# Both ends of a two-layer hybrid decode step rewritten: tokens in column halves ahead of the weights, last norm tile by tile

## The chip, the cores and the metric

One core of one Trainium2 chip runs the whole kernel. The metric is the device time of one execution in microseconds (us). The engines are PE (TensorE, matmuls; PEld is its weight load), DVE (VectorE), ACT (ScalarE), POOL (GpSimd) and SP (SyncE, which issues DMAs here). A matmul reads 128x128 stationary weights and a moving operand of up to 280 columns, the tokens.

## The reference, cut to what matters

A stack of two layers works on 272 prompt positions (16 of them meta tokens) and 8 decoded tokens, 280 columns, at width 1024. Each layer is a feed-forward block, three mixers side by side (S5, RWKV7, RG-LRU), and a second feed-forward block. The ends are what the change touches:

```python
meta = broadcast_to(meta_tokens, (bp, 16, 1024));  xp = concatenate([meta, x_prompt]);  xs = x_sample
for l in range(2):                       # for xp and xs alike
    h = h + 0.5 * swiglu(rmsnorm(h, ffn1_norm), w_gate, w_up, w_down)     # 1024 -> 2816 -> 1024
    h = h + mixers(rmsnorm(h, mix_norm) @ w_in) @ w_out
    h = h + 0.5 * swiglu(rmsnorm(h, ffn2_norm), w_gate2, w_up2, w_down2)
y_prompt = rmsnorm(xp, final_norm)[:, 16:];  y_sample = rmsnorm(xs, final_norm)
# rmsnorm(x, g) = x * rsqrt(mean(x*x) + 1e-6) * g
```

## The kernel before, in words

Activations lie transposed: width on the partitions in eight tiles j (KD = 8), tokens on the free axis. `hres` is the residual (8 tiles of 128x280, f32). For exactness every f32 operand is split in two parts of the type f32r: the activation into `xh` (made by ACT, times the norm's gain) and the residue `xl` (DVE), a weight piece of 128x4x128 into `whi` (ACT, L191) and `wlo` (DVE, L192). One product of a 128x128 weight block is three matmuls, xh by whi (L200), xl by whi (L201) and xh by wlo (L202). The reciprocal norm of a token is applied behind the product, so that a gemm needs the gains only.

Weights are loaded piece by piece (`wpiece`, L188, 256 KB from SP) into rings of five staging buffers, five whi and four wlo. A feed-forward block runs over 22 tiles of gate and up products, and then over eight output tiles j of the down product, each 66 matmuls of 264 columns in the last layer, where the meta tokens are left out (`ffn`, L313). After each the residual is added (L355, L356), its Square is added to `acc` (`acc_sq`, L257 to L261) and the next operand is split (`split_x`, L264, L265).

At the start five DMAs load the tokens as rows (L295 to L299), SP's three and ACT's two queues before the weights. The gains `pvst` are loaded and transposed to `pv` (`load_params`, L223 to L232). For each tile j the PE transposes the tokens into one PSUM bank (L306), DVE copies the bank into hres (L307), and `split_x` reads hres. PSUM has eight banks: psa three, psb two, psc two, psd one; a bank is free once its last reader is done. At the end ("fin", L1550 to L1575) six sums over partitions by `ones` (L1557) give the norm of each token, ACT scales the residual by the gain (`hg`, L1564), PE transposes it back (L1570), DVE multiplies by the norm (`yo`, L1571), and three DMAs store the rows.

A scheduler with a timeline model sets the order of instructions on each engine; `issue_after` ties one behind another. DMAs that SP and ACT issue share eight completion lanes in turn: an issue waits until the DMA eight before it has landed.

## Time and profile before

| | us |
|---|---|
| median of 3 runs | 1263.94 (1262.67 to 1265.52) |
| profiled execution | 1258.64, span 1256.8 |
| PE busy | 1211.6 (96% of the span) |
| DVE busy | 971.9 (77%) |
| ACT busy | 698.0 (56%) |
| POOL busy | 214.4 (17%) |
| chain that ended last | PE 83%, DVE 8%, DMA 4%, POOL 2%, issue 2%, ACT 1% |

The profile is of one execution; its span is the time from the first to the last recorded event. Busy shares are means over the whole span, and the two ends of a program have limits of their own, so the rows below are read by stretch. In rows of the timeline the first number is the start in us, the second the duration, then come the engine, the line, the operation, what is written and read, the tile and the count; in brackets stands the idle time of the engine ahead of it and what ended it. Consecutive matmuls overlap in these rows: the distance of two starts is the time that one costs.

### The profile page before, as it was taken

The numbers are of one execution on the slowest core, as the hardware profiler recorded it, in microseconds if no ns is written. First come the engines' busy times: TensorE is split into PE (matmuls) and PEld (weight loads), VectorE is DVE, ScalarE is ACT, GpSimd is POOL, SyncE is SP. The second block draws the span as 40 slices with busy tenths as digits, with TensorE's granted clock in tenths as the row PEclk, the third lists the DMA queues.
The fourth block names the chain that finished last, engine by engine and source line by source line (L and its number), as shares of the span: only waits on it lengthen the run. The fifth ranks groups of instructions, "written<-read, shape, count | busy, mean of one in ns | idle before, by whom it ended". The sixth has DMA issues, their size and how long they took to land.

```text
span 1256.8 us, 29154 instructions
## 1 busy us (share of the span) xinstructions
PE 1211.6 (96%) x10744; PEld 1154.9 (92%) x10744; DVE 971.9 (77%) x2345; ACT 698.0 (56%) x1529; POOL 214.4 (17%) x385
## 2 busy tenths in 40 slices
PE   7999999999898999999999999999999989999996
PEld 6999999988776999999998999998898779999996
DVE  7899957779687789985877778666876778877864
ACT  4466677564365556668544555457633656455543
POOL 2000000143443210000025000001615332500000
PEclk9999999989897999999999999999995989999998
DMA  7665654523311766554579656564423038965662
GB/s 184 170 184 161 178 145 142 164 83 107 96 29 55 187 165 183 171 170 129 155 203 240 184 169 171 171 176 128 119 79 82 2 87 226 244 196 170 190 187 83
DMA packets 376908, 187.47 MB, mean 149 GB/s; under 512 B 45532, under 2 KB 375352, under 8 KB 376766
## 3 DMA queue, kind: packets, MB, share of 16 engines
q1 hardware_dynamic: 376430, 184.47, 52.8%
q8 instruction: 84, 1.38, 0.5%
q10 hardware_dynamic: 336, 1.15, 0.3%
q14 instruction: 58, 0.48, 0.1%
HBM read 181.31 MB, written 3.37 MB: 147 GB/s over the span
## 4 chain that ended last, share of the span: by engine, by line
PE 83%; DVE 8%; DMA 4%; POOL 2%; issue 2%; ACT 1%; SPq 1%; DVEq 0%; ACTq 0%; POOLq 0%
PE psa L202 11%; PE psa L201 11%; PE psa L200 11%; PE psc L201 6%; PE psc L202 6%; PE psc L200 6%; PE psb L202 6%; PE psb L201 6%; PE psb L200 6%; PE psc L756 1%; DVE wlo L192 1%; PE psc L719 1%; PE psc L681 1%; PE psb L901 1%; DMA bc<-ds 1%
## 5 line engine op out<-in xcount | busy, mean ns | idle before, releaser
L191 ACT ACTIVATE whi<-stg 128x512 fp32r<-128x512 f32 (+2 forms) x664 | 400.7, 609 | 383.2 <-PE psa L201 101.3
L192 DVE TENSOR_TENSOR wlo<-stg,whi 128x512 fp32r<-128x512 f32 (+2 forms) x640 | 432.6, 682 | 129.2 <-ACT whi L191 29.9
L202 PE MATMUL psa<-xh,wlo 128*128 128x280 f32 (+1 forms) x930 | 274.1, 296 | 2.4 <-DVE wlo L192 2.3
L200 PE MATMUL psa<-xh,whi 128*128 128x280 f32 (+1 forms) x930 | 272.7, 294 | 2.0 <-DVE ts L1300 2.0
L201 PE MATMUL psa<-xl,whi 128*128 128x280 f32 (+1 forms) x930 | 273.0, 294 | 0.0
L202 PEld LDWEIGHTS psa<-xh,wlo 128*128 128x128 f32 x930 | 176.4, 190 | 6.0 <-DVE wlo L192 3.5
L200 PEld LDWEIGHTS psa<-xh,whi 128*128 128x128 f32 x930 | 177.1, 191 | 4.2 <-DVE ts L1300 2.2
L201 PEld LDWEIGHTS psa<-xl,whi 128*128 128x128 f32 x930 | 176.8, 190 | 1.6 <-issue 0.7
L201 PE MATMUL psc<-xl,whi 128*128 128x280 f32 (+1 forms) x498 | 144.6, 291 | 1.2 <-DVE xl L265 0.7
L202 PE MATMUL psc<-xh,wlo 128*128 128x280 f32 (+1 forms) x498 | 145.0, 291 | 0.7 <-DVE wlo L192 0.5
L200 PE MATMUL psc<-xh,whi 128*128 128x280 f32 (+1 forms) x498 | 144.8, 291 | 0.8 <-ACT xh L264 0.4
L202 PE MATMUL psb<-xh,wlo 128*128 128x280 f32 (+1 forms) x396 | 114.8, 290 | 1.0 <-DVE wlo L192 1.0
L200 PE MATMUL psb<-xh,whi 128*128 128x280 f32 (+1 forms) x396 | 115.0, 290 | 0.0
L201 PE MATMUL psb<-xl,whi 128*128 128x280 f32 (+1 forms) x396 | 114.8, 290 | 0.0
L201 PEld LDWEIGHTS psc<-xl,whi 128*128 128x128 f32 x498 | 94.0, 189 | 2.0 <-DVE xl L265 1.1
L202 PEld LDWEIGHTS psc<-xh,wlo 128*128 128x128 f32 x498 | 93.9, 188 | 1.7 <-DVE wlo L192 1.5
L200 PEld LDWEIGHTS psc<-xh,whi 128*128 128x128 f32 x498 | 93.9, 189 | 1.5 <-ACT xh L742 0.8
L202 PE MATMUL psb<-hh,wlo 128*128 128x280 f32 (+1 forms) x264 | 76.8, 291 | 0.0
L201 PE MATMUL psb<-hl,whi 128*128 128x280 f32 (+1 forms) x264 | 76.7, 291 | 0.0
L202 PE MATMUL psa<-hh,wlo 128*128 128x280 f32 (+1 forms) x264 | 76.5, 291 | 0.1
L200 PE MATMUL psb<-hh,whi 128*128 128x280 f32 (+1 forms) x264 | 76.7, 290 | 0.0
L201 PE MATMUL psa<-hl,whi 128*128 128x280 f32 (+1 forms) x264 | 76.6, 290 | 0.0
(620 smaller groups left out, 2578.7 us busy)
## 6 DMA issues: line engine op xcount, KB each, us to landing
stg<-in_ffn_w_gate_dram SPq DMA_DIRECT2D x176, 256.0 KB
stg<-in_ffn_w_up_dram SPq DMA_DIRECT2D x176, 256.0 KB
stg<-in_ffn_w_down_dram SPq DMA_DIRECT2D x160, 256.0 KB
stg<-in_w_in_dram SPq DMA_DIRECT2D x72, 256.0 KB
stg<-in_w_out_dram SPq DMA_DIRECT2D x32, 192.0 KB
bc<-ds SPq DMA_DIRECT2D x24, 192.0 KB
stg<-in_ffn_w_down_dram SPq DMA_DIRECT2D x32, 128.0 KB
bc<-ds SPq DMA_DIRECT2D x12, 256.0 KB
```

The costliest lines, as they stand in the source:

```text
L191: S.activation(hi[:, :kc], st[:, :kc], AF.Copy)
L192: (eng or V).tensor_tensor(lo[:, :kc], st[:, :kc], hi[:, :kc].bitcast(F32), op=SUB)
L200: PE.matmul(out, w[wk[i]][0], ah[:, k], start=(first and i == 0), stop=False)
L201: PE.matmul(out, w[wk[i]][0], al[:, k], start=False, stop=False)
L202: im = PE.matmul(out, w[wk[i]][1], ah[:, k], start=False, stop=(last and i == n - 1))
L681: PE.matmul(px[r][:, a], s5['xbt'][:, 4 * T + a, r], u4[:, 4 * T + a, 8:16 + NQ], start=True, stop=True)
L719: PE.matmul(py[32 * i:32 * i + 32, c0:c0 + n], w, x[:, o:NQ + ND], start=(m == 0), stop=(m == 2), skip_group_check=True, tile_position=(0, ...
L756: PE.matmul(pz[:, :NT], gw[k][:, j], z5[:, k, 0:NT], start=(k == 0), stop=(k == 2))
L901: PE.matmul(pg[h][:, hp], BK[r0, hp, c - 1].rearrange("p a t -> p (a t)"), RA[r0, hp, i, cs], start=True, stop=True)
```

## The change

At the start, the tokens are loaded by column halves, the first halves and the gains first, the weights behind the second halves. Nine matmuls of `ones` by itself into a psd bank run ahead of the transposes. xh (ACT) and xl (DVE) read the tokens' bank in PSUM, and the copies into hres come later: tile 0 behind the sixth xl, the other seven tied behind the wlo of the first four weight pieces, which are now made here and handed to the first `ffn` as `first`. The cast of `cidx` moves into `s5_prepare`, and the transposed final gain (`fgain`) goes.

At the end, "fin" becomes `final_norm`, which the last `ffn` calls. The final gain is loaded as a row broadcast to 128 partitions (`fg`, 512 KB) and scaled by POOL. After each output tile j of the last down product ACT squares the residual, PE adds three sums of one column over all eight tiles in one psd bank, and transposes the tile into three psa banks, four tiles to a bank; after tile 3 DVE multiplies the first half of the banks by fg. After tile 7 come the root, the scaling of the first halves (ACT) and the product of the second halves (DVE); four DMAs of 256 KB and a small one store the rows. The down product takes its banks from psb and psc in turn there, and the last `acc` isn't added up.

```diff
-        nc.sync.dma_start(xt[0][0:16], D['meta_tokens'])
-        nc.sync.dma_start(xt[0][16:128], xp[0:112])
-        nc.scalar.dma_start(xt[1], xp[112:240])
-        nc.scalar.dma_start(xt[2][0:16], xp[240:256])
-        nc.scalar.dma_start(xt[2][16:24], D['x_sample'].rearrange("b s d -> (b s) d"))
-        for _ in load_params(xin, PV_SPEC[:1]):
+        for c in (slice(0, DM // 2), slice(DM // 2, DM)):
+            nc.sync.dma_start(xt[0][0:16, c], D['meta_tokens'][:, c])
+            nc.sync.dma_start(xt[0][16:128, c], xp[0:112, c])
+            nc.scalar.dma_start(xt[1][:, c], xp[112:240, c])
+            if c.start == 0:
+                nc.scalar.dma_start(xt[2][0:16], xp[240:256])
+                nc.scalar.dma_start(xt[2][16:24], D['x_sample'].rearrange("b s d -> (b s) d"))
+                pv0 = load_params(xin, PV_SPEC[:1])
+                next(pv0)
+        pt = psD()
+        for _ in range(9):
+            PE.matmul(pt[:, :P], ones, ones, start=True, stop=True)
+        for _ in pv0:
             pass
...
         for j in range(KD):
             pt = psAB()
             for i, r in enumerate(rows):
                 PE.transpose(pt[:, P * i:P * i + r], xt[i][:r, P * j:P * j + P], ident[:r, :r])
-            V.tensor_copy(hres[:, j, :], pt[:, :NT])
-            split_x(j, gvec(0, 'ffn1_norm'), ALLC)
+            S.activation(xh[:, j], pt[:, :NT], AF.Copy, scale=g0[:, j:j + 1])
+            V.scalar_tensor_tensor(xl[:, j], pt[:, :NT], g0[:, j:j + 1], xh[:, j].bitcast(F32), op0=MUL, op1=SUB)
+            pts.append(pt)
+            if j == 5:
+                V.tensor_copy(hres[:, 0], pts[0][:, :NT])
+        for i in range(4):
+            w, iv = wpiece(wgu[i % 2][:, 4 * (i // 2):4 * (i // 2) + 4, 0:P], last=True)
+            first[i % 2] += w
+            for j in range(2 * i + 1, min(2 * i + 3, KD)):
+                with tc.issue_after(iv.ins):
+                    V.tensor_copy(hres[:, j], pts[j][:, :NT])
...
+    def final_norm():
+        groups = [(16, 128), (144, 128), (272, 8)]
+        fg = s5t.tile([P, DM], F32, name="fg", tag="k0")
+        nc.sync.dma_start(fg, D['final_norm'].unsqueeze(0).to_broadcast([P, DM]))
+        G.tensor_scalar(fg, fg, KR, None, op0=MUL)
...
+        def step(j):
+            sq = tmp("f", NRK)
+            S.activation(sq[:, 16:NT], hres[:, j, 16:], AF.Square)
+            for i, (c0, n) in enumerate(groups):
+                PE.matmul(ss[:n, i:i + 1], sq[:, c0:c0 + n], ones[:, 0:1], start=(j == 0 and i == 0), stop=(j == KD - 1),
+                          skip_group_check=True)
+            if j % 4 == 0:
+                pt[:] = [psA() for _ in groups]
+            for i, (c0, n) in enumerate(groups):
+                PE.transpose(pt[i][:n, P * (j % 4):P * (j % 4) + P], hres[:, j, c0:c0 + n], ident)
+            if j == 3:
+                for i, (c0, n) in enumerate(groups):
+                    V.tensor_tensor(yo[i][:n, half[0]], pt[i][:n], fg[:n, half[0]], op=MUL)
+            if j < KD - 1:
+                return
+            V.tensor_scalar(v[:, 0:2], ss[:, 0:2], 1e-6, None, op0=ADD)
+            V.tensor_scalar(v[:ND, 2:3], ss[:ND, 2:3], 1e-6, None, op0=ADD)
+            rsq(v, ry, rz)
+            for i, (c0, n) in enumerate(groups):
+                S.activation(yo[i][:n, half[0]], yo[i][:n, half[0]], AF.Copy, scale=ry[:n, i:i + 1])
+                V.scalar_tensor_tensor(yo[i][:n, half[1]], pt[i][:n], ry[:n, i:i + 1], fg[:n, half[1]], op0=MUL, op1=MUL)
+                for h, q in zip(half, (nc.scalar, nc.sync)):
+                    if i < 2:
+                        q.dma_start(yp[c0 - 16:c0 - 16 + n, h], yo[i][:n, h])
+            nc.sync.dma_start(ysm, yo[2][:ND])
...
-        acc2 = new_acc()
+        acc2 = new_acc() if gnext is not None else None
...
-                pd = psAB()
+                pd = psAB() if tail is None else (psB, psC)[j & 1]()
...
-                acc_sq(j, acc2, cols)
-                if gnext is not None:
+                if tail is None:
+                    acc_sq(j, acc2, cols)
                     split_x(j, gnext, cols)
+                else:
+                    tail(j)
```

How the instructions stand now is shown at three places. First SP at the start, before (xt are the tokens, pvst the gains, stg a weight piece, lw small weights of a mixer):

```order
L295 DMA xt_129<-in_meta_tokens_dram 16x1024
L296 DMA xt_129<-in_x_prompt_dram 112x1024
L223 DMA pvst_137<-in_ffn_norm_dram 8x2x128
L188 DMA stg<-in_ffn_w_gate_dram 128x4x128 x2
L188 DMA stg<-in_ffn_w_up_dram 128x4x128 [waits DMAHW0_49]
L188 DMA stg<-in_ffn_w_up_dram 128x4x128 [waits DMAHW1_49]
L188 DMA stg<-in_ffn_w_gate_dram 128x4x128 [waits DMAHW2_49]
L400 DMA lw<-in_rwkv_w_up_dram 64x384 [waits DMAHW3_49]
```

SP at the start, now:

```order
L289 DMA xt_127<-in_meta_tokens_dram 16x512
L290 DMA xt_127<-in_x_prompt_dram 112x512
L220 DMA pvst_135<-in_ffn_norm_dram 8x2x128
L289 DMA xt_127<-in_meta_tokens_dram 16x512
L290 DMA xt_127<-in_x_prompt_dram 112x512 [waits DMAHW0_49]
L187 DMA stg<-in_ffn_w_gate_dram 128x4x128 [waits DMAHW1_49]
L187 DMA stg<-in_ffn_w_up_dram 128x4x128 [waits DMAHW2_49]
L187 DMA stg<-in_ffn_w_gate_dram 128x4x128 [waits DMAHW3_49]
L187 DMA stg<-in_ffn_w_up_dram 128x4x128 [waits DMAHW4_49]
L187 DMA stg<-in_ffn_w_gate_dram 128x4x128 [waits DMAHW5_49]
```

The two weight pieces that went out without a wait now stand behind the second token halves, and each waits for a lane (DMAHW and a number). ACT issues its token loads, three before and four now, ahead of all its other work.

Second, DVE behind its constants, before (hres<- is the copy from PSUM):

```order
L151 CAST cidx<-cidxI 128x21
L192 TENSOR_TENSOR wlo<-stg,whi 128x512 x3
L232 COPY pv<-psd 128x8 x2
L307 COPY hres<-psb 128x280
L307 COPY hres<-psc 128x280
L307 COPY hres<-psa 128x280
L307 COPY hres<-psb 128x280
L192 TENSOR_TENSOR wlo<-stg,whi 128x512
L307 COPY hres<-psc 128x280
L307 COPY hres<-psa 128x280 x2
L265 SCALAR_TENSOR_TENSOR xl<-hres,pv,xh 128x280
```

The same place now, up to the copy that frees the bank (psc) that the first gemm writes:

```order
L226 COPY pv<-psd 128x8 x2
L312 SCALAR_TENSOR_TENSOR xl<-psb,pv,xh 128x280
L315 COPY hres<-psb 128x280
L312 SCALAR_TENSOR_TENSOR xl<-psc,pv,xh 128x280
L312 SCALAR_TENSOR_TENSOR xl<-psa,pv,xh 128x280
L312 SCALAR_TENSOR_TENSOR xl<-psb,pv,xh 128x280
L312 SCALAR_TENSOR_TENSOR xl<-psc,pv,xh 128x280
L312 SCALAR_TENSOR_TENSOR xl<-psa,pv,xh 128x280
L191 TENSOR_TENSOR wlo<-stg,whi 128x512
L322 COPY hres<-psc 128x280
```

The residues moved ahead of the copies, and the first weight piece's wlo behind six residues.

Third, PE at the end of the program, before (hg is the scaled residual, acc the squares' sum):

```order
L1570 MATMUL psa<-ident,hg 128x128
L1570 MATMUL psc<-ident,hg 128x128
L1570 MATMUL psa<-ident,hg 8x128
L1557 MATMUL psb<-ones,acc 128x1 x2
L1557 MATMUL psb<-ones,acc 8x1
L1570 MATMUL psb<-ident,hg 128x128 x4
```

PE now, in the middle of the last output tile's 66 matmuls, where the tile before it is finished:

```order
L201 MATMUL psc<-hh,wlo 128x264
L350 MATMUL psa<-ident,hres 128x128 x2
L350 MATMUL psa<-ident,hres 8x128
L199 MATMUL psc<-hh,whi 128x264
L200 MATMUL psc<-hl,whi 128x264
L345 MATMUL psd<-ones,tf 128x1 x2
L345 MATMUL psd<-ones,tf 8x1
L201 MATMUL psc<-hh,wlo 128x264
```

Three transposes and three sums of one tile now stand between the matmuls of the next, for tiles 0 to 6; the six of tile 7 are PE's last instructions. On POOL the scaling of fg stands between two steps of the second layer's S5 path that stood next to each other, behind a copy of an output state that now comes after them.

## Rows read from the trace of the kernel before

**Rows 1.** Busy time by stretches: stretch, us, each engine's busy us (count), granted clock.

```profile
0.00:20.00 20.00, 11.27 (x56) 10.07 (x57) 15.29 (x37) 11.00 (x24) 8.85 (x35) 1.00 0.78 191
1220.00:1240.00 20.00, 20.00 (x167) 20.00 (x166) 11.52 (x22) 8.53 (x16) 0.00 (x0) 1.00 0.45 132
```

**Rows 2.** Timeline of the first 19 us: SP, PE and DVE.

```profile
4.88 0.92 SPq L188 DMA_DIRECT2D stg<-in_ffn_w_up_dram  x2
7.35 0.66 PE L306 MATMUL psb<-ident,xt 128*128 128x128 f32 x2 [7.35 <-DMA xt<-in_x_prompt_dram]
10.50 0.38 PE L230 MATMUL psd<-ident,pvst 8*128 8x8 f32 x2
11.22 0.23 DVE L232 COPY pv<-psd 128x8 f32<-128x8 f32 x2
13.21 0.60 PE L200 MATMUL psc<-xh,whi 128*128 128x280 f32 x1 [0.43 <-ACT xh L264]
15.02 0.60 PE L201 MATMUL psc<-xl,whi 128*128 128x280 f32 x1 [0.73 <-DVE xl L265]
18.22 0.33 PE L201 MATMUL psc<-xl,whi 128*128 128x280 f32 x1
```

**Rows 3.** Chain that ended last, 0 to 30 us: start, us, what.

```profile
16.09 0.23 PE psa L201
...
20.08 0.13 PE psc L202
```

**Rows 4.** Timeline of DVE at the start: residues and a wlo.

```profile
12.80 0.68 DVE L192 TENSOR_TENSOR wlo<-stg,whi 128x512 fp32r<-128x512 f32 x1
...
17.65 1.33 DVE L265 SCALAR_TENSOR_TENSOR xl<-hres,pv,xh 128x280 fp32r<-128x280 f32 x3
```

**Rows 5.** DMA queues, 0 to 4 us: packets, MB, share; q10 is ACT's, q1 SP's.

```profile
q10 hardware_dynamic: 131, 0.52, 37.4%
q1 hardware_dynamic: 39, 0.09, 9.2%
```

**Rows 6.** Timeline of PE: sums and transposes inside streams of matmuls.

```profile
1055.34 0.63 PE L278 MATMUL psd<-ones,acc 128*128 128x1 f32 x6
...
1056.13 0.28 PE L200 MATMUL psc<-xh,whi 128*128 128x264 f32 x1
...
159.69 0.60 PE L637 MATMUL psd<-ident,bx 128*128 128x128 f32 x4
...
160.26 0.28 PE L201 MATMUL psb<-hl,whi 128*128 128x280 f32 x1
```

**Rows 7.** Timeline of the end, from the last gemm matmul to the stores.

```profile
1242.58 0.28 PE L202 MATMUL psb<-hh,wlo 128*128 128x264 f32 x1
...
1243.36 0.43 DVE L356 TENSOR_TENSOR hres<-tf,hres 128x264 f32<-128x264 f32 x1
...
1245.81 0.41 ACT L260 ACTIVATE tf<-hres 128x264 f32<-128x264 f32 x1
...
1247.06 0.63 PE L1557 MATMUL psb<-ones,acc 128*128 128x1 f32 x6
...
1249.90 0.75 DVE L1571 TENSOR_SCALAR yo<-psc,ry 128x512 f32<-128x512 f32 x1
...
1251.38 0.36 SPq L1573 DMA_DIRECT2D out_dram<-yo  x1
```

**Rows 8.** DMA from 1240 to 1257 us in 40 slices of 0.425 us.

```profile
GB/s 0 0 0 0 0 0 0 0 0 0 0 0 0 0 0 0 0 0 0 0 0 0 0 0 0 0 0 0 116 405 395 386 395 434 376 39 0 0 0 0
```

**Rows 9.** Timeline of the second mixers: POOL, and DVE's step before the S5 product.

```profile
1010.69 0.80 POOL L729 TENSOR_TENSOR tf<-tf 128x280 f32<-128x280 f32 x1
...
1013.78 0.44 DVE L731 SCALAR_TENSOR_TENSOR u<-tf 128x280 f32<-128x280 f32 x1
```

**Rows 10.** Chain, 380 to 420 us, and busy time of 397 to 398.

```profile
392.86 4.74 PE psc L756 x10
...
397.00:398.00 1.00, 1.00 (x6) 0.45 (x5) 0.69 (x2) 0.36 (x1) 0.00 (x0) 0.92 0.64 191
```

62 lines of the change are left out of this document (22 added, 40 removed).

## The prediction, made blind

> **What bounds the kernel now.** I read the busy time by stretches first. TensorE (PE) works 20.00 us of the 20 us from 1220 on, and 11.27 in the first 20 us [rows 1]. So PE is the bound in the feed-forward blocks, and two kinds of edit count at the ends: those that let the stream of matmuls start earlier or finish sooner, and those that put instructions into a stretch where PE has no idle time, which cost their full PE time there.
>
> Then the start, in order of time. SyncE's (SP) third weight load is issued at 4.88, since it waited for a token load to land. The first transpose runs at 7.35, when the tokens are there; the norm's gains (pvst) are transposed at 10.50 and copied from 11.22; the first gemm matmul starts at 13.21, does three matmuls, and the stream is only continuous from 15.02, where a matmul had waited 0.73 us for the residue xl [rows 2]. It runs at the lower clock at first: the chain of waits has a 280-column matmul every 0.23 us at 16.09 and every 0.13 us at 20.08 [rows 3], and the rows of the timeline change from the one to the other at 18.22 [rows 2]. These are the two levels, 280 columns at 1.2 and at 2.4 GHz. Sixteen matmuls stand before that change, so they cost 16 x 0.105 = 1.7 us more than at the upper level. Had the stream been continuous, it would have begun at 18.22 - 16 x 0.233 = 14.5, less 0.1 for its slower first matmul: 14.4. That is the number that the front has to beat.
>
> Last the end. From the start of the last gemm matmul at 1242.58 to the end of the span, 1256.8, are 14.22 us: the residual's add, a Square behind seven scalings on ACT (ScalarE), an add, the sums at 1247.06, the reciprocal root, six scalings from PSUM on DVE (VectorE) from 1249.90, and the stores, of which the first is issued at 1251.38 [rows 7].
>
> **The sum is made against the profiled execution**, 1258.64 us with a span of 1256.8; the median of the runs shown is 1263.94, 5.3 us above, and I take the same difference over to it.
>
> **Front: when the first operand is there.** The tokens' first halves (32 and 224 KB on SP, 256 KB on ACT), the 24-row tile and the gains are some 0.61 MB. The trace of before moves 0.61 MB by 4.0 us, both queues together [rows 5], and the end of the kernel shows 1.85 us from the last byte (1254.95, the last filled slice) to the end of the span [rows 8]. So they land at 5.85 if they go first. The row speaks against that: ACT's queue q10 had 0.52 MB by 4.0 us, SP's q1 0.09 [rows 5], so that ACT's second half, 256 KB, can go ahead of SP's first; at the 0.4 MB a us of the stores [rows 8] this is 0.65 us more, 6.5. The Trainium skill, DMA: Bandwidth & Descriptors, section Queues, rings and completion order, says that a DMA engine serves its queue rows in turn; by that they would land together at 5.85, and the trace here shows it only in part. I take 6.2, between the ends, because ACT's first half has a start of one issue in both kernels.
>
> On the same page, section Bandwidth, there is a rule that speaks against halving the loads: 1 MiB or more per DMA for three quarters of the peak. Its table has 138 GB/s at 64 KB and 341 at 1 MB; an estimate between them, 250 GB/s for 256 KB, would put the landing 0.8 us later and the whole sum 0.8 us higher. No row here has a load of 256 KB with 2 KB rows alone.
>
> From 6.2 the PE does eight transposes of 128 columns at 0.22 (fourteen from 7.35 to 10.50 [rows 2]), four of 24 columns, 0.4 in all, then the gains, whose copy starts 0.72 us after their transposes [rows 2]: 6.2 + 1.8 + 0.4 + 0.7 = 9.1 for the first xh. The first xl follows 0.5 later (an xh takes a little more than an xl), and DVE works through the order shown: six xl, a copy, the first wlo, and the copy that frees the bank of the first gemm. The eight of 280 columns cost 0.44 each (1.33 for three), the wlo 0.6 to 0.7 [rows 4]: 9.1 + 0.5 + 3.5 + 0.6 = 13.7. The second halves are due before 9.1 + 0.5 + 4 x 0.44 = 11.4, with the fifth xl; SP issues its own only when a lane is free, as at 4.88 before [rows 2], thus data by 6.6 and landing near 8.6: hidden. The weight pieces come after that; 256 KB at 0.9 us each, the first lands near 10, its whi is due on ACT after six xh, at 9.1 + 6 x 0.44 = 11.7: hidden, with 1.5 us in hand. The residual's copies and the sums of squares then lie beside a full PE. So the stream starts **0.7 us earlier** (14.4 - 13.7).
>
> The nine warm-up matmuls of ones are f32, two passes each, between 1 and 6 us, where PE has nothing else to do. Whether they change the clock, I bound from both sides: if it is up for all sixteen matmuls, 1.7 us are gained and the transposes before run at half, another 1.1; if the pause of over 4 us between the last transposes and the first gemm undoes it, nothing. Rows speak for both: in the mixer of layer 0 ten groups of such f32 matmuls from 392.86 run 4.74 us at the lower level, and in the slice at 397 the granted clock is 0.92 [rows 10], so this kind of work raises it; but the transposes of before, 7.35 to 12.5, were followed by a first gemm at the lower level [rows 2, 3]. I take half of the 1.7. **Front: -0.7 - 0.85 = -1.55 us**, from 0 to -0.7 - 1.7 - 1.1 = -3.5.
>
> **Last down projection.** For each of tiles 0 to 6 the change puts three sums of one column and three transposes between the next tile's matmuls, as the order shows. PE has no idle time there [rows 1], so they cost what they take. Three sums of the same form (six records) in a 264-column stream: from their start at 1055.34 to the matmul at 1056.13 are 0.79 us, and one other matmul, 0.12, lies between: 0.67 us. Four transposes, read in the same way: 159.69 to 160.26 is 0.57, less 0.12: 0.45, three 0.34 [rows 6]. Together 1.0 a tile, **+7.05 us for seven**, from 5.7 (0.3 for three transposes and 0.5 for the sums, without the hand-over) to 7.6 (0.63 and 0.45). Nothing waits for them: hres is ready 1.2 us after a tile's last matmul, its Square 1.7 (below), and they are queued half a tile, 4 us, later. The dropped DVE adds and ACT scalings gain nothing, since both engines had idle time there (DVE 11.52 of 20 [rows 1]).
>
> **Tail.** From the last gemm matmul's start: hres added at +1.21 (1243.36 + 0.43), Square, which now stands right behind it, 0.41 (1245.81 before): +1.7 and the sums start. Before, 2.84 us passed from the sums' start to the first product from PSUM (1247.06 to 1249.90), with three adds, the root's eight steps and a scaling; now there is one add and the scaling less, 0.1 and 0.2: +4.25. The product takes 0.75: +5.0 for the first SP store, while ACT scales its half beside it. Before, the first store was issued at 1251.38, +8.8 [rows 7]. Then the same 1.08 MB at 0.4 MB a us [rows 8]: data from +5.75 (the trace of before has the first bytes 0.8 after the issue) to +8.45, and 1.85 us: +10.3 in place of 14.22. **-3.9 us**, from -3.0 (the small store last) to -4.5.
>
> **Second mixers.** The POOL (GpSimd) now scales the 128x1024 gains before two steps of the path to the second S5 product. A 280-column operation takes 0.80 there, so it costs at most 1024/280 x 0.80 = 2.9, and I count it from nothing up. Most is hidden: POOL's last step ended at 1011.49, an activation of about 0.45 takes its result, and the DVE step behind that came only at 1013.78, so some 1.8 us are in hand [rows 9]. I take +0.4, from 0 to +1.0. The gains' load has idle DMA queues there.
>
> **Sum:** -1.55 + 7.05 - 3.9 + 0.4 = +2.0 us: 1260.6 for the profiled execution, **1265.9 on the median**. Its own range is 1263.5 to 1268.
>
> **The rivals.** Warm clock: front -3.5, the sum +0.05, 1264.0. For it speaks [rows 10], against it the pause.
>
> Faster: beside the warm clock, half of the inserted work is hidden, since a sum is one column and its cost is nearly all weight load, which runs beside matmuls. Then 7 x 0.5 = 3.5 and the sum is -3.5 + 3.5 - 3.9 + 0.4 = -3.5: 1260.4. Against it speak [rows 6], where the same insertions cost their full time. It decides below 0.6 us a tile.
>
> Slower: the weights are late. All pieces now wait for tokens to land, five of them one lane after another; if the first whi starts after 12 (1.5 us in hand used up) and each of the next comes 1 us late, the stream stalls at its first pieces, front +1.5 in place of -1.55: the sum +5.05, 1269.0. For it speaks SP's wait at 4.88 [rows 2].
>
> The change doesn't do what it says: the first gemm is no earlier, and the clock is low when it starts. Front 0, the sum +3.55, 1267.5.
>
> **How the numbers follow.** Forecast 0.42, warm clock 0.20, faster 0.17, weights late 0.14, front without effect 0.07. About 0.2%, 2.5 us (1261.4 to 1266.5), is what a measurement of this kernel can tell from no change. The forecast's range lies two thirds within it and one third or a little more above, the warm clock's nearly all within: faster 0.20, same 0.42, slower 0.38. The range reaches from 1260.0, the faster rival, to 1269.5, the late weights.
>
> **What would show it.** In the trace of after: first xh near 9.1, first gemm near 13.7 and without gaps behind it, spacing 0.23 or 0.13 there; whi of the first piece near 11.7; between the matmuls of the last down projection a loss of 1.0 us at each of seven tiles; about 10.3 us from the last tile's last matmul to the end; the second S5 product at most 1 us later behind its mixer. I am wrong if the seven insertions cost less than 0.6 each, or if the mixers, which the scheduler has reordered in a few rows, move by over 2 us.

## The result, and the profile after

| | before | after |
|---|---|---|
| median, us | 1262.67 (1259.68 to 1265.52, 5 runs) | 1272.45 (1269.24 to 1275.8, 5 runs) |
| ratio to before | | 1.0084 (95%: 1.0061 to 1.0106) |
| span of the profiled execution | 1256.8 | 1269.7 |

The change makes the kernel slower, by 7.7 to 13.4 us of 1262.67. The prediction was 1265.9, 1260.0 to 1269.5: too low, and the time lies outside its range. Of its terms the last down projection and the tail came out nearly as worked out; the front gained even more than was said, and none of it reached the end.

First the page of after, engines and the chain's shares. The table ahead of the prediction has 1211.6 us for PE:

```profile
PE 1223.1 (96%) x10804; PEld 1165.1 (92%) x10804; DVE 964.3 (76%) x2336; ACT 696.0 (55%) x1524; POOL 217.3 (17%) x385
...
PE 84%; DVE 7%; DMA 5%; ACT 2%; issue 1%; POOL 1%; SPq 0%; DVEq 0%; ACTq 0%
```

PE is busy 11.5 us more, in a span 12.9 us longer.

**The start.** Timeline of after, PE and ACT, to be held against [rows 2]:

```profile
1.12 4.21 PE L300 MATMUL psd<-ones 128*128 128x128 f32 x18 [1.12 <-DVE ones L114]
...
5.57 0.41 PE L310 MATMUL psb<-ident,xt 128*128 128x128 f32 x2 [0.24 <-DMA xt<-in_x_prompt_dram]
...
7.34 0.49 ACT L311 ACTIVATE xh<-psb,pv 128x280 fp32r<-128x280 f32 x1 [3.34 <-DVE pv L226]
...
7.89 0.60 PE L310 MATMUL psc<-ident,xt 128*128 128x128 f32 x3 [0.78 <-DMA xt<-in_x_prompt_dram]
...
11.93 0.57 PE L199 MATMUL psc<-xh,whi 128*128 128x280 f32 x1 [1.04 <-ACT xh L311]
...
15.09 0.43 PE L200 MATMUL psa<-xl,whi 128*128 128x280 f32 x1
...
15.33 0.35 PE L199 MATMUL psc<-xh,whi 128*128 128x280 f32 x1
```

The first halves of the tokens are there at 5.57 (forecast 6.2), the first xh starts at 7.34 (9.1) and the first gemm matmul at 11.93 (13.7; 13.21 before). The clock follows in the windows of after (stretch, us, each engine's busy us and count, granted clock, DMA share, GB/s):

```profile
5.20:8.60 3.40, 2.37 (x20) 1.82 (x19) 0.97 (x4) 1.26 (x4) 1.55 (x11) 1.00 1.02 272
...
8.80:15.20 6.40, 5.36 (x22) 4.42 (x22) 6.40 (x16) 5.95 (x15) 2.98 (x4) 0.50 0.72 187
...
1200.00:1220.00 20.00, 20.00 (x170) 19.80 (x169) 9.33 (x17) 8.47 (x15) 0.00 (x0) 1.00 0.62 181
```

The nine warm-up matmuls raise the clock for the transposes (1.00 from 5.2 to 8.6, the level of 2.4 GHz). Then PE stands for 0.78 us, since the second halves of the tokens land only at 7.89, and from 8.8 to 15.2 the clock is 0.50, the level of 1.2 GHz: the last transposes run there, and with them the first fourteen matmuls of the stream, up to the row at 15.33, behind which the steps are 0.13 us in place of 0.23. Before there were sixteen. The last window, from 1200 to 1220, belongs to the down projection: PE is busy for all of its 20 us.

**The last down projection.** Timeline of PE in after, one tile's insertion:

```profile
1200.11 0.28 PE L200 MATMUL psc<-hl,whi 128*128 128x264 f32 x1
1200.23 0.49 PE L350 MATMUL psa<-ident,hres 128*128 128x128 f32 x3
1200.47 0.37 PE L201 MATMUL psc<-hh,wlo 128*128 128x264 f32 x1
1200.68 0.63 PE L345 MATMUL psd<-ones,tf 128*128 128x1 f32 x6
1201.23 0.39 PE L199 MATMUL psc<-hh,whi 128*128 128x264 f32 x1
1201.46 0.28 PE L200 MATMUL psc<-hl,whi 128*128 128x264 f32 x1
```

From the first to the last of the four gemm matmuls are 1.35 us, where three steps of 0.12 would be 0.36: 1.0 us for this tile, the predicted price.

**The tail.** Timeline of after from the last gemm matmul, to be held against [rows 7]:

```profile
1258.91 0.28 PE L201 MATMUL psc<-hh,wlo 128*128 128x264 f32 x1
...
1260.17 0.42 ACT L343 ACTIVATE tf<-hres 128x264 f32<-128x264 f32 x1 [7.87 <-DVE hres L413]
...
1260.64 0.73 PE L345 MATMUL psd<-ones,tf 128*128 128x1 f32 x6
...
1263.24 2.06 DVE L361 SCALAR_TENSOR_TENSOR yo<-psa,nrm,fg 128x512 f32<-128x512 f32 x3
...
1264.02 1.02 SPq L364 DMA_DIRECT2D out_dram<-yo  x2
```

The sums start 1.73 us after the last matmul, the first product at 4.33, the first SP store is issued at 5.11, and the span ends at 10.8 (1269.7 - 1258.91); before these were 4.48, 7.32, 8.80 and 14.22 [rows 7]. The stores' bytes, DMA of after from 1255 to 1270 us in 40 slices of 0.375 us:

```profile
GB/s 0 0 0 0 0 0 0 0 0 0 0 0 0 0 0 0 0 0 0 0 0 0 0 0 0 0 240 399 355 377 393 371 388 350 11 0 0 0 0 0
```

They run from 1264.75 to 1267.75, 5.8 to 8.8 us behind the last matmul (forecast 5.75 to 8.45), and 1.95 us pass from there to the end.

**Where the time went.** The kernels compute the same 7584 gemm matmuls, so I count them from the first, matmul 0, and compare the time at which the n-th starts, in each trace (us from the span's start, as in the timeline). Matmul 1655 is the last of the first feed-forward block, 2015 the last of the first w_in product, 5807 of the second w_in, 7055 the last ahead of the last down projection.

| stretch, us | before | again | front alone | tail alone | after | again |
|---|---|---|---|---|---|---|
| first gemm matmul at | 13.21 | 13.27 | 11.71 | 13.26 | 11.93 | 12.01 |
| 0 to 100 | 16.5 | 17.3 | 15.4 | 16.0 | 15.2 | 15.5 |
| 100 to 1655 | 212.6 | 212.6 | 216.4 | 212.5 | 213.5 | 214.8 |
| matmul 1655 at | 242.3 | 243.2 | 243.4 | 241.8 | 240.6 | 242.2 |
| 1655 to 2015 | 78.4 | 75.4 | 75.9 | 76.9 | 77.4 | 75.4 |
| first mixers' end | 78.1 | 84.6 | 84.1 | 83.1 | 81.7 | 82.2 |
| 2016 to 5447 | 461.8 | 462.3 | 464.7 | 463.5 | 464.9 | 467.4 |
| 5447 to 5807 | 76.0 | 77.0 | 76.0 | 78.5 | 76.0 | 78.4 |
| second mixers' end | 83.5 | 79.7 | 85.7 | 83.1 | 85.7 | 82.3 |
| 5808 to 7055 | 158.4 | 159.5 | 159.7 | 162.3 | 161.5 | 162.8 |
| 7055 to 7583 | 64.07 | 64.07 | 64.07 | 71.16 | 71.11 | 71.11 |
| last gemm matmul to the end | 14.2 | 15.7 | 14.1 | 10.6 | 10.8 | 10.8 |

The trace that the prediction was made from has the shortest first mixers of all: 78.1, where the seventeen others of this study have 80.8 to 85.0. Of the 12.9 us between the two spans 3.6 are that.

### The profile page after: what moved, and what is told of

It is laid out like the page before. It is cut to its first block, busy times and chain, and to the rows that moved or that the text cites. A ratio compares the mean times of both kernels' runs of the same rounds, so it can differ in the third digit from the quotient of the medians.

```text
span 1269.7 us, 29260 instructions
## 1 busy us (share of the span) xinstructions
PE 1223.1 (96%) x10804; PEld 1165.1 (92%) x10804; DVE 964.3 (76%) x2336; ACT 696.0 (55%) x1524; POOL 217.3 (17%) x385
## 4 chain that ended last, share of the span: by engine, by line
PE 84%; DVE 7%; DMA 5%; ACT 2%; issue 1%; POOL 1%; SPq 0%; DVEq 0%; ACTq 0%
PE psa L201 11%; PE psa L200 10%; PE psa L199 10%; PE psc L201 7%; PE psc L200 7%; PE psc L199 7%; PE psb L201 6%; PE psb L200 6%; PE psb L199 6%; DMA stg<-in_ffn_w_gate_dram 2%; PE psc L779 1%; DVE wlo L191 1%; PE psc L741 1%; PE psb L961 1%; PE psc L816 1%
## 5 line engine op out<-in xcount | busy, mean ns | idle before, releaser
L191 DVE TENSOR_TENSOR wlo<-stg,whi 128x512 fp32r<-128x512 f32 (+2 forms) x640 | 431.6, 681 | 133.9 <-ACT whi L190 30.3
L201 PE MATMUL psb<-hh,wlo 128*128 128x280 f32 (+1 forms) x286 | 83.4, 292 | 0.2 <-DVE wlo L191 0.2
L199 PE MATMUL psb<-hh,whi 128*128 128x280 f32 (+1 forms) x286 | 83.2, 291 | 0.3 <-ACT whi L190 0.3
L200 PE MATMUL psb<-hl,whi 128*128 128x280 f32 (+1 forms) x286 | 82.9, 290 | 0.0
L201 PEld LDWEIGHTS psb<-xh,wlo 128*128 128x128 f32 x396 | 74.3, 188 | 1.6 <-DVE wlo L191 1.6
L199 PEld LDWEIGHTS psb<-xh,whi 128*128 128x128 f32 x396 | 74.5, 188 | 0.0
```

The lines of the kernel that those rows point to most:

```text
L191: iv = (eng or V).tensor_tensor(lo[:, :kc], st[:, :kc], hi[:, :kc].bitcast(F32), op=SUB)
L199: PE.matmul(out, w[wk[i]][0], ah[:, k], start=(first and i == 0), stop=False)
L200: PE.matmul(out, w[wk[i]][0], al[:, k], start=False, stop=False)
L201: im = PE.matmul(out, w[wk[i]][1], ah[:, k], start=False, stop=(last and i == n - 1))
```

## Experiments

Three theories stood against one another. **T1:** the front's lead is lost in the first feed-forward block, where the weights are handed over at DVE's pace, whenever PE starts. **T2:** the tail pays a second time outside its own stretch, by the scaling of the gain on POOL (GpSimd) or by another order of the mixers. **T3:** neither edit does it; dropping `fgain` moves every later tile in SBUF by 32 bytes, and DMAs run slower for it.

**Each end by itself.** The front alone keeps before's end, the section "fin" (diff against after):

```diff
-                else:
-                    tail(j)
...
-                pd = psAB() if tail is None else (psB, psC)[j & 1]()
+                pd = psAB()
...
+    with tc.tile_pool(name="fin", bufs=1) as fp:
```

> The front of the change alone; the last norm is that of the kernel before. In the two traces the stream of gemm matmuls runs 3.0 us earlier after the front, but the first layer's mixers take 3.6 us more and some feed-forward stretches lose 0.6 to 1.4 us each. Theory A (order): the front's other order of instructions in the first layer causes the mixers' loss each time, so this kernel is -3.0 + 3.6 + about 2 = 2 to 3 us slower than before. Theory B (chance): mixers and stretches vary from run to run whatever the kernel, so this kernel is 3 us faster, ratio 0.9975, and its first mixers may take 78 or 82 us.

Measured 1265.92 us, 1.0026 of before (1.0005 to 1.0046): +3.3 us, 0.6 to 5.8. The prediction's -1.55 is excluded.

The tail alone puts `final_norm` on the kernel before and leaves its start as it was (diff against after):

```diff
-        for c in (slice(0, DM // 2), slice(DM // 2, DM)):
-            nc.sync.dma_start(xt[0][0:16, c], D['meta_tokens'][:, c])
...
+        nc.sync.dma_start(xt[0][0:16], D['meta_tokens'])
+        nc.sync.dma_start(xt[0][16:128], xp[0:112])
```

> The tail of the change alone; the start is that of the kernel before. Down projection +7.05 and tail -3.5 are in both theories. Theory A (order, with the scaling of the final gain on POOL in the second mixers): second mixers +2.2 and the stretches behind them up to +2.5, so 6 to 8 us slower than before. Theory B (chance): 3.5 us slower, ratio 1.003.

Measured 1270.31, 1.0047 (1.0023 to 1.0071): +5.9 us, 2.9 to 9.0, where the prediction's three terms make +3.55, which lies within that interval. The two ratios together make 1.0073, after's is 1.0084: the ends add up, and no interplay is needed.

Both kernels once more, for a second trace of each (no edit):

> The kernel before again, for a second trace. Theory A (order): both mixers take 78.1 and 83.6 us between the gemms around them as in the first trace, to 0.5 us, and the clock's low stretches lie in the same places. Theory B (chance): they differ from the first trace by 2 us or more.

> The changed kernel again, for a second trace. Theory A (order): both mixers take 81.7 and 85.7 us as in the first trace, to 0.5 us. Theory B (chance): they differ from it by 2 us or more.

Measured 1263.32 and 1274.33; their stretches are the columns "again". The first mixers are shorter in before by 3.6 us in the one pair and longer by 2.4 in the other, so they tell nothing of the change.

**T1: the front's lead.** The front alone starts matmul 100 at 27.1 us, 2.7 earlier than the kernel before (29.7), and has lost that at matmul 1655 (243.4 and 242.3). The waits of PE from 15 to 250 us by what was waited for (in total, times, longest), first before:

```profile
PE psa L202 <- DVE wlo L192: 0.6, 1, 0.6
```

and the front alone:

```profile
PE psa L201 <- DVE wlo L191: 2.3, 3, 1.4
...
PE psb L201 <- DVE wlo L191: 0.9, 2, 0.7
PE psb L199 <- ACT whi L190: 0.3, 1, 0.3
```

PE waits 2.9 us more for weights being split. The longest, in the timeline of the front alone (POOL, DVE, PE):

```profile
51.35 1.41 POOL L434 MEMSET sta<- 32x1536 f32 x1 [37.19 <-DVE stsh_in L438]
...
51.35 1.43 DVE L464 TENSOR_SCALAR smlr<-pv 128x2 f32<-128x2 f32 x1
...
51.78 1.28 DVE L191 TENSOR_TENSOR wlo<-stg,whi 128x512 fp32r<-128x512 f32 x2
...
52.88 0.40 PE L201 MATMUL psa<-xh,wlo 128*128 128x280 f32 x1 [1.36 <-DVE wlo L191]
```

A DVE operation of two elements a partition takes 1.43 us: it starts and ends with POOL's clearing of `sta`, and the wlo that PE waits for stands behind it. The Trainium skill, Trainium Architecture — The Big Picture, section What this means for kernel authors, says that DVE and GpSimd share a port pair under an exclusive lock; the two rows that start together at 51.35 agree, 1.43 and 1.41 us.

So I cleared `sta` once a layer in place of five times, on the front and on the kernel before:

```diff
+        sta = tp.tile([32, 12, 4, 32], F32, name="sta", tag="sta")
+        G.memset(sta, 0.0)
...
-            a = tp.tile([32, 12, 4, 32], F32, name="sta", tag="sta")
-            G.memset(a[:, :nt], 0.0)
+            a = sta
```

> The front alone, and the staging tile of the decode state (sta) cleared by POOL once a layer in place of five times. In the eight traces with the front the stretch from the 100th to the 700th gemm matmul takes 79.3 to 82.4 us, with one to three stalls of 0.9 to 1.7 us where POOL's memset of sta (1.4 us) and a DVE step of two elements that takes 1.43 us lie side by side and the next wlo comes late; in the five without it 79.6 to 79.8, with one such stall. Theory (the memsets hold DVE up, and the front's order puts them where a wlo is due): 78.4 to 79.3 here, and the lead of 2.7 us at the 100th matmul is kept to the 1000th. Rival (the order itself, other DVE steps ahead of wlo): 81 or more, and the lead is gone by the 700th.

> The kernel before with the one memset of sta a layer, as the measure for the run with the front. Theory (memsets): 78.4 us from the 100th to the 700th in place of 79.7, total 1 to 2 us faster, ratio 0.999. Rival: 79.7 as before, no difference.

Measured 1263.74, 1.0008 (0.9989 to 1.0027) with the front, and 1261.47, 0.9998 (0.9975 to 1.0021) without. From matmul 100 to 700 the kernel before goes from 79.7 to 78.5 us (79.6 to 79.8 in seven traces without the front, 78.5 in both with a single clearing). With the front it goes from 82.2 to 81.0, but traces of the front with five clearings lie from 79.3 to 82.2 there, so that step could be chance. What the runs do show is that with a single clearing the front still takes 81.0 and 81.2. The clearing is a cost of both kernels and not what makes the front lose. (With the edit the scheduler also writes DVE's steps in another order.) What is left with the front, timeline of DVE and PE of that run:

```profile
49.16 2.17 DVE L440 STREAM_TRANSPOSE stsh_in<-sta 32x352 f32<-32x352 f32 x4
...
51.44 0.16 DVE L466 TENSOR_SCALAR smlr<-pv 128x2 f32<-128x2 f32 x1
...
51.87 1.28 DVE L191 TENSOR_TENSOR wlo<-stg,whi 128x512 fp32r<-128x512 f32 x2
...
52.60 0.40 PE L201 MATMUL psa<-xh,wlo 128*128 128x280 f32 x1 [0.94 <-DVE wlo L191]
```

The operation that took 1.43 us beside the clearing takes 0.16 without it, but PE still waits for the wlo behind it. The kernel before has the same four transposes of the states, in the timeline of DVE:

```profile
45.76 2.17 DVE L419 STREAM_TRANSPOSE stsh_in<-sta 32x352 f32<-32x352 f32 x4
...
48.47 1.28 DVE L192 TENSOR_TENSOR wlo<-stg,whi 128x512 fp32r<-128x512 f32 x2
```

and there no matmul waits behind them. The pace there is DVE's, as the windows show, first of before:

```profile
60.00:110.00 50.00, 50.00 (x390) 49.94 (x389) 48.66 (x204) 29.67 (x55) 0.60 (x2) 1.00 0.64 182
```

and the front alone:

```profile
60.00:110.00 50.00, 49.09 (x378) 48.79 (x379) 48.40 (x202) 28.81 (x54) 1.06 (x3) 1.00 0.62 176
```

DVE works 48.7 and 48.4 of these 50 us, in both kernels. It makes the wlo and does the state transposes and scalings of the mixers besides; PE is full too in before, but with the front it does 12 matmuls fewer in the same time, since it waits. From the end of a piece's wlo to the start of the first matmul that reads it, the first four pieces have 5.9 to 8.6 us before and 1.1 to 2.7 with the front; from the eighth to the fifteenth piece both have 3.5 to 5.1; and between the 24th and the 32nd both come down to 0.1. Two facts together speak for DVE: a start that is 2.8 us earlier for PE at matmul 100 is gone by matmul 1655 (242.6 on the mean of seven traces with the front, 242.5 of seven without, all with five clearings; the first trace of after alone still has 1.7 us there), while the four clearings that no longer hold up DVE shorten the way from matmul 100 to 1655 by 1.3 +- 0.4 us, by a fit over all 18 traces, with and without the front. And the loads aren't late there: from 60 to 110 us DVE waits 1.4 us in all with the front, none of it for a piece of weights. So the traces bear T1 out for this part: PE is fed at DVE's pace, and PE's start doesn't set it. It isn't shown by itself, since the scheduler also wrote DVE's steps in another order with the front, and no run has the one without the other. (Which of DVE's other steps the front makes PE wait for differs from trace to trace; no run moved them one by one.)

That covers about 1.7 us of the loss, up to matmul 700 (108.6 on the mean with the front, 109.7 without: 1.1 of the lead are left). The rest, 1.2, lies from matmul 1000 to 1500: 74.9 to 75.0 us with the front as the change has it, 73.6 before, with the same 78 matmuls and transposes of other kinds in between, which the scheduler put at other places. DVE isn't full there (50.47 of 65 us before, from 110 to 175). Three waits for pieces being split (wlo, whi, wlo) are 0.7 us of it, in each trace of this front, and before has none; why these come late is open.

**The clock.** What the front could gain from it, two runs show. One takes the nine warm-up matmuls away:

```diff
-        pt = psD()
-        for _ in range(9):
-            PE.matmul(pt[:, :P], ones, ones, start=True, stop=True)
```

> The front alone without the nine warm-up matmuls. Theory (they gain time only on the transposes, since the clock falls again before the first gemm): transposes of 128 columns take 0.21 in place of 0.11, the first gemm starts 1 us later than with them, near 12.7, and the 20th 1 us later too, near 17. Rival (they matter for the stream): the clock rises 2 us or more later, the 20th at 18 or later.

The other adds fourteen where PE would pause, behind the transposes of tiles 3, 6 and 7:

```diff
+            if j in (3, 6, 7):
+                fill({3: 4, 6: 4, 7: 6}[j], it)     # so many PE.matmul(hb[:, :P], ones, ones)
```

> The front alone, with 14 more matmuls of ones between and behind the transposes, so that PE does not pause for over 1 us before the first gemm. In the trace of the front alone the granted clock rises at 5.2 us behind the nine warm-up matmuls, falls at 8.7 and rises again at 15.4, and the first sixteen gemm matmuls run at the lower level. Theory (the pause costs the clock): the clock stays up, the 20th gemm matmul starts 4.4 us behind... that is 2.6 us after the first in place of 4.4, near 14.3. Rival: it falls all the same, and the 20th starts near 16.1 or later.

Without the warm-up 1264.97, with the fourteen 1266.35, a single run each; times so close tell nothing, the traces do. The windows of the second, where after has a clock of 0.50:

```profile
8.80:15.20 6.40, 6.40 (x49) 5.76 (x49) 6.40 (x16) 5.86 (x15) 2.98 (x4) 1.00 0.83 228
```

PE is busy throughout and the clock stays at its upper level, 2.4 GHz. Matmul 20 of the stream starts at 17.50 without the warm-up, at 16.1 to 16.5 in five traces with it and at 15.3 to 15.5 in three with the fourteen; before it starts at 18.76. So the warm-up is worth 1.0 to 1.4 us, mostly on the transposes (the first gemm starts at 12.98 without it and at 11.7 to 12.2 with it), and holding the clock 0.6 to 1.2 more. But matmul 1655 starts at 243.8, 243.4 and 242.3 in these three kernels, before at 242.3 and 243.2: what an earlier start gains at matmul 20 is not there any more.

**T2 and T3: the tail.** First 32 bytes put back where `fgain` stood. The order of instructions on every engine is that of the tail alone:

```diff
+    pad = const.tile([P, KD], F32, name="pad")
+    V.memset(pad, 0.0)
```

> The tail alone with one unused tile of 32 bytes a partition put where the removed final gain (fgain) stood. The order of instructions is that of the tail alone on every engine; only addresses in SBUF differ: without fgain every later tile lies 32 bytes lower, the broadcast state tiles (bc2) at 198112 in place of 198144. In the three traces with the tail the 1024-byte packets of the stretches with those loads take 68 to 75 ns (640 to 700 us) against 60 to 65 in the three without, the 512-byte packets beside them 33 to 34 against 31. Theory layout: with the 32 bytes back both are as before, the second feed-forward of layer 0 takes 256 us of 258 and the run of the last one up to its down products 159.5 of 162, so the kernel is 1 to 2 us slower than before in place of 5.9. Theory order: nothing of that changes, 5 to 6 us slower.

The same two lines added to the kernel before, and to the change:

> The kernel before with one unused tile of 32 bytes a partition, so that every later tile lies 32 bytes higher (bc2 at 198176); the order is that of before on every engine. Theory layout: packets of 1024 bytes take 68 to 75 ns in the stretches with broadcast state loads, and the kernel is 4 to 5 us slower, ratio 1.0035. Theory order: no difference, ratio within 1.001.

> The whole change with the unused 32 bytes where fgain stood; order as in the change. So far the tail with the 32 bytes had the shorter packets and 255.2 and 159.6 us in the second feed-forward of layer 0 and in the last one up to its down products, against 257.9 and 162.3 without them at the same order, but its median moved only by 2 us of 1270; the kernel before with 32 bytes more had longer packets and no other time. Theory layout: 256 and 159.5 us here, against 258.2 to 259.4 and 161.5 to 162.8 in the two traces of the change, and 4 to 5 us less in all, ratio to before 1.004 to 1.005 in place of 1.0084. Rival: the stretches shorten by under 1 us each and the ratio stays over 1.007.

Measured: tail 1268.4, 1.0056 (1.0035 to 1.0077), against 1270.31 and 1.0047 without; before 1262.81, 1.0008 (0.9983 to 1.0032); after 1272.13, 1.0085 (1.0063 to 1.0106), against 1272.45 and 1.0084. The traces do show an effect. DMA queue of the tail alone, 648 to 693 us, where weights and the RWKV states are loaded (packets, MB, share of 16 engines):

```profile
q1 hardware_dynamic: 20310, 9.68, 100.3%
```

and the tail with the 32 bytes, the same stretch:

```profile
q1 hardware_dynamic: 21487, 10.35, 92.8%
```

In the second, 7% more is moved in a smaller share of time; the kernel before has 10.28 MB at 92.1% from 645 to 690. A packet of 512 bytes takes 33.8 ns on the mean from 640 to 700 us in the tail alone, 31.1 with the 32 bytes, 30.9 before; the four traces with moved tiles have 32.7 to 34.3, the fourteen others 30.3 to 32.0. The Trainium skill, DMA: Bandwidth & Descriptors, section How a descriptor splits into AXI transactions, says of the transactions that read a descriptor's data that they must start on a multiple of 256 bytes, and that a descriptor which doesn't start there costs extra beats. Here the side that moved is the tile that is written, which the section doesn't speak of. Dropping `fgain` moves the broadcast state tile from byte 198144 of a partition, a multiple of 256, to 198112, and the packets go the way of that rule. But the time doesn't follow: against the kernel before, the 32 bytes change the tail from 1.0047 to 1.0056 and the change from 1.0084 to 1.0085, and the kernel before isn't measurably slower with the shift. T3 is real in the packets and not shown in the time.

Then the scaling of the gain behind the mixers: its tile is taken from the last feed-forward block's pool, so that it can't start before, with the 32 bytes kept:

```diff
-        fg = s5t.tile([P, DM], F32, name="fg", tag="k0")
+        fg = hp.tile([P, DM], F32, name="fg")
```

> The tail with the 32 bytes, its gains' tile taken from the last feed-forward's own memory: load and scaling then stand behind the second mixers, whose order on PE, DVE, ACT and POOL is that of before. In the four traces with the tail the last part of the second mixers, from the last gate matmul (psc<-tf,lg) to the first gemm behind them, takes 24.7 to 25.7 us, in the four with before's order of it 22.1 to 22.4, one with 23.7 and one with 24.1 where the clock was low for 17 of them. Theory (gains in the mixers): 22.2 to 23.7 here, and 2 to 3 us less than the 1.0056 of the tail with 32 bytes, ratio 1.003. Rival (chance of the clock): 25 again, ratio 1.0056.

Measured 1267.61, 1.0047 (1.0026 to 1.0068). What it took away, timeline of POOL in after:

```profile
1011.09 3.31 POOL L331 TENSOR_SCALAR fg<-fg 128x1024 f32<-128x1024 f32 x1
...
1014.74 1.24 POOL L789 TENSOR_TENSOR tf<-ta,gb 128x280 f32<-128x280 f32 x1
1015.94 0.80 POOL L789 TENSOR_TENSOR tf<-tf 128x280 f32<-128x280 f32 x1
```

and the chain of after, where the second S5 product starts:

```profile
1019.28 0.37 DVE u L791
...
1019.69 2.24 PE psc L816 x4
```

Before, POOL's last step ended at 1011.49 and DVE's step for the product at 1014.22 [rows 9], 2.7 us later. In after POOL's last step ends at 1016.74 and DVE's is done 2.9 us later; in the run with the late scaling the two are 1013.19 and 1016.25, 3.1 apart. What the prediction had as 1.8 us in hand didn't take up the scaling. The last part of the mixers, from the last matmul that reads `lg` (the RG-LRU gates' weights) to the first of w_out, takes 24.5 to 25.7 us in the five traces with the scaling there, 23.9 with it late, and 23.7 to 24.3 in four with before's order and a similar time at the lower clock. By the traces the scaling costs about 1.2 us; the medians, 0.8 apart (1268.4 and 1267.61), can't tell that from nothing.

The rest of that stretch is the clock. Windows of the mixers' end, before:

```profile
1004.00:1020.00 16.00, 11.87 (x44) 7.92 (x43) 14.75 (x55) 9.81 (x22) 5.10 (x9) 0.68 0.06 18
```

and after:

```profile
1008.00:1027.00 19.00, 13.73 (x47) 8.77 (x46) 15.81 (x62) 9.34 (x23) 8.06 (x10) 0.52 0.04 11
```

The granted clock is 0.68 and 0.52. Kernels with before's order in this part take 22.1 to 22.5 us where 10 of them are at the lower level, and 23.7 to 24.3 where 14 to 18 are: 1.6 us, which kernels without the tail lose too. But all six traces with the tail have 16 to 19 us at the lower level there, 17.9 with the late scaling, while of the twelve others four have 14 to 17 and eight 10. Whether the tail brings the lower clock about, no run shows.

**Another tail.** If the insertions cost PE time and the short chain at the end gains, the two can be parted: squares are added up as before, ACT scales hres in place by the gain tile by tile, and all transposes and the three sums stand behind the last gemm matmul; halves are scaled by ACT and DVE and stored in four pieces:

```diff
+            acc_sq(j, acc2, slice(16, NT))
+            S.activation(hres[:, j, 16:], hres[:, j, 16:], AF.Copy, scale=fgain[:, j:j + 1])
+            if j < KD - 1:
+                return
...
+            for jj in range(KD):
+                for i, (c0, n) in enumerate(groups):
+                    PE.transpose(pt[i][jj // 4][:n, P * (jj % 4):P * (jj % 4) + P], hres[:, jj, c0:c0 + n], ident)
```

> Another tail on the kernel before: no PE instruction inside the last down products. After each output tile ACT squares it and DVE adds it up as before, and ACT scales the residual by the gain at once, in place; all transposes and the sums stand behind the last gemm, and the two halves of each row block are scaled by ACT and DVE side by side and stored by four DMAs. fgain and so the addresses stay. Theory of the sum: the last 528 gemm matmuls take 64.1 us as before, in place of 71.1 with the change, and the end from the last of them 10.5 us in place of 14.2: 3.7 us faster, ratio 0.997. Rival: ACT's scalings hold up whi, so that the 528 take over 65 us and the gain is gone.

Measured 1257.83, 0.9959 (0.9936 to 0.9983): faster than both kernels. Timeline of its end:

```profile
1245.38 0.28 PE L202 MATMUL psb<-hh,wlo 128*128 128x264 f32 x1
...
1247.79 0.63 PE L329 MATMUL psd<-ones,acc 128*128 128x1 f32 x6
...
1250.36 0.75 DVE L339 TENSOR_SCALAR yo<-psa,nrm 128x512 f32<-128x512 f32 x1
1251.13 1.02 SPq L342 DMA_DIRECT2D out_dram<-yo  x2
```

The first store is issued 5.75 us after the last matmul, 0.64 later than in after, and the last down projection takes 64.07 us as before. Of the change's gain at the end, 3.0 of 3.4 us are had without the 7 us (14.2 to 11.2; by itself a ratio of 0.9976, within the interval).

Three more with this tail: on the front with the fourteen matmuls, with the single clearing, and with all three:

> The front with the 14 more matmuls of ones that kept the clock up (its 20th gemm matmul started at 15.2 us, 3.5 before that of the kernel before) and the other tail (ACT scales the residual tile by tile, no PE work inside the last down products), which alone came to 0.9959. By the sum: front -3.5 at the start, of which 2 to 3.5 are lost again in the first feed-forward, and -3.8 for the tail, so 4 to 6 us faster than before, ratio 0.9955 to 0.997. Rival: the front's loss in the first feed-forward goes beyond its gain, ratio 0.998 or above.

> The other tail (nothing of PE's inside the last down products) with the one memset a layer, the start of before. Theory: 3.8 us by the tail and 1 to 2 by the memsets, ratio 0.9955 to 0.996. Rival: the memsets count for nothing, 0.997.

> The front with the 14 more matmuls, the other tail and the one memset a layer. Theory (memsets take the front's lead): with them gone 3 us of the start are kept beside the tail's 3.8, ratio 0.994 to 0.995. Rival (the front costs by its order): no better than the other tail with the start of before, ratio 0.997 or above.

Measured 1264.22, 1.0013 (0.9986 to 1.0041); 1257.69, 0.9975 (0.9952 to 0.9998); 1261.63, 0.9987 (0.9968 to 1.0006). In each pair the kernel with the front is the slower one by its median, and the clearing adds nothing that can be measured. The best kernel of this study is before's start with this tail.

## Why the prediction was wrong

| term, us | predicted | measured |
|---|---|---|
| front | -1.55 (0 to -3.5) | +3.3 alone (0.6 to 5.8) |
| last down projection | +7.05 (5.7 to 7.6) | +7.04 |
| tail | -3.9 (-3.0 to -4.5) | -3.4 |
| second mixers | +0.4 (0 to 1.0) | about +1.2 for the scaling |
| stretches between | no term | about +3 with the tail |

**Right.** The price of an insertion into a full PE, worked out from [rows 6], was 7.05 and is 7.04 (64.07 to 71.11), the same in every trace that has it. The tail ended 10.8 us behind the last matmul in place of 10.3, since the stores took 3.0 us for 2.7. That is 3.4 us of gain between these two traces; on the mean the six traces with this tail have 10.7 and the eight with before's 14.4: 3.7, nearly the 3.9 forecast.

**The front: the step that failed** is "The residual's copies and the sums of squares then lie beside a full PE. So the stream starts 0.7 us earlier". Up to the stream's start the working erred on the careful side: a least-squares fit over all 18 traces (front, tail and single clearing as factors) puts matmul 100 earlier by 2.9 +- 0.3 us. Of the clock the forecast had half of 1.7 us on the stream's first matmuls; these ran nearly all at the lower level still, fourteen for sixteen, and the 1.0 to 1.4 us that the warm-up gained lie mostly on the transposes ahead of them. The tokens and the first xh were earlier than forecast. What failed is that a lead at the start counts to the end. The same fit has the front lose 3.2 +- 0.3 from matmul 100 to 1655. The sentence took PE's 20.00 of 20 us at 1220, where DVE has 11.52 [rows 1], for the state of every feed-forward block; from 60 to 110 us the kernel before has PE at 50.00 and DVE at 48.66 of 50, and a PE that comes earlier there waits for the weights that DVE hands over. The rival "weights late" was the nearest, a stream that stalls on weights, but it put the cause on their loads and stood at +1.5 with a chance of 0.14.

Behind matmul 1655 the front costs another 3 us or so by its own median; by the fit it is w_in (1.7 +- 1.0), matmuls 2016 to 5447 (1.7 +- 0.6) and the second mixers (0.7 +- 1.0) that are longer with it. These stretches are not touched by the edit, and in the first two every engine has the same instructions in the same order with and without the front; only within the mixers a few stand in another order. What w_in has comes from the three traces with the fourteen extra matmuls (81.1 to 82.1 us); the six others with the front lie where those without it do, 75.4 to 78.4, by the time they have at the lower clock (0 to 6.8 us). From 2016 to 5447 it is waits again, as the waits of PE in that stretch show, first before:

```profile
PE psa L202 <- DVE wlo L192: 1.3, 2, 1.1
PE psb L202 <- DVE wlo L192: 1.0, 2, 0.7
```

and after:

```profile
PE psa L201 <- DVE wlo L191: 1.9, 2, 1.6
PE psc L201 <- DVE wlo L191: 1.8, 3, 0.9
PE psa L199 <- ACT whi L190: 1.1, 1, 1.1
```

With the shorter ones, the waits for weights being split are 2.5 us before and 5.4 after, 2.8 and 6.3 in the second traces, and 5.1 in the front alone. Not every kernel with the front has more: the change with 32 bytes has 4.2, the five others 1.8 to 3.2, and the nine traces without the front 1.1 to 3.9. Why the weights come later, at an unchanged order, I have not found.

**The mixers: mis-sized.** The scaling took 3.31 us (bound 2.9), and the 1.8 us "in hand" behind POOL's last step didn't take it up. **The sum** had no term for what lies between the ends. With the tail, matmuls 5808 to 7055 take 2.0 +- 0.5 us longer and 5447 to 5807 1.3 +- 0.6. The latter goes with the clock: 75.4 to 77.3 us with up to 3.4 us at the lower level, 78.4 with 6.8, in kernels with and without the tail. With the 32 bytes put back the former is 159.6 in the tail alone (162.3 without) and 159.6 in the change (161.5 and 162.8 without), but 161.2 with the late scaling, which has the 32 bytes too and its load of the gains in this stretch; and the ratios didn't come down, 1.0056 for 1.0047 and 1.0085 for 1.0084. The clock has a part here as well: five of the six traces with the tail have 0.8 to 6.0 us of this stretch at the lower level, of the twelve others one. Whether the shift of the tiles is this loss stays open.

**The base.** The profiled execution of before had lucky mixers, 78.1 us where the others have 80.8 or more. The difference between its time and the median, which the prediction took over as it was, holds for both kernels and did no harm; a comparison of the two traces alone would have charged the change 3.6 us too much. The prediction's own sign of being wrong, mixers that move by over 2 us, did come (81.7 for 78.1 and 85.7 for 83.5), but a second trace of the unchanged kernel moves by as much (84.6 and 79.7), so it is a sign of nothing here.

## What to carry to other kernels

An earlier start of the bound engine is worth only what its feeders have in hand: before counting a lead to the end, look for the first stretch behind it where a second engine is full as well (here DVE, 48.66 of 50 us), since the lead can end there, as it did here. Work pushed into a stretch where an engine has no idle time costs its full time at each place and can be priced to a few per cent from the same instructions elsewhere in the trace, so take the shorter chain at the end without it: sums kept on the engines with idle time, transposes in one block behind the last matmul. Before two traces are subtracted stretch by stretch, take a second one of each: a stretch that differs by 4 us between two runs of one program explains nothing of an edit.

## What the runs showed of the hardware

- The length of a program's mixers varies with the granted clock, in any kernel: in the first mixers, 37.5 to 51.2 us at the lower level in seventeen traces and 30.7 in the one with the shortest, 78.1 us in place of 80.8 to 85.0. Thirty-five runs of the kernel before on one chip spread from 1253.97 to 1267.27.
- An operation on DVE of two elements a partition took 1.43 us while POOL cleared a tile for 1.41 us, and 0.16 us in a run without that clearing. Clearing once in place of five times gains 1.2 us from matmul 100 to 700 in the kernel before, of which its medians show nothing.
- Moving SBUF tiles by 32 bytes, with every instruction in the same place, changed the mean time of a 512-byte packet from 33.8 to 31.1 ns and the queue's share from 100.3% to 92.8%.
- With nine warm-up matmuls of ones (eighteen records, 1.12 to 5.33 us) the granted clock was 1.00 from 5.2 to 8.6 us, under the first transposes, where without them the upper level first came at 17.1. PE stood for 0.78 us up to 7.89; the clock was at the lower level from 8.6, in the midst of the next transposes, to 15.5. In the front with a single clearing it fell only at 11.9, and with fourteen more matmuls of ones in the gaps it was 1.00 throughout.
- The kernel before with 32 bytes more, so that its tiles are moved the other way, has the slower packets too (33.1 ns for 512 bytes) and the same median (1.0008).
